# The end of a one-core encoder layer: its last layer norms written in a hand-made order on VectorE

## The chip, the core and the metric

The kernel runs on one core of one Trainium2 chip. TensorE multiplies matrices into PSUM, VectorE and ScalarE work on tiles of 128 partitions in SBUF, GpSimd issues gathers, and SyncE issues most of the transfers. The metric is the device time of one execution in microseconds. Lower is better.

## The reference

One encoder layer over 512 tokens of width 1024. The end of it is what matters here: a feed-forward part that picks 128 of 16384 experts for each token, a gated embedding, and a layer norm over their sum. Everything before is attention and routing.

```python
def layer_norm(x, g, b):
    mu = jnp.mean(xf, axis=-1, keepdims=True)
    var = jnp.mean(jnp.square(xf - mu), axis=-1, keepdims=True)
    y = (xf - mu) * lax.rsqrt(var + LN_EPS)
    return y * g + b
...
    # in peer_ffn, for each token:
    hpre = jnp.einsum('td,ted->te', xb, u_table[idx])
    act = g * jax.nn.gelu(hpre, approximate=False)
    return jnp.einsum('te,ted->td', act, v_table[idx])
...
    ffn = peer_ffn(h, ...)
    ple = gate * (p[i] @ ple_w[i])
    h = layer_norm(DN_ALPHA * h + ffn + ple, ln2_g, ln2_b)
```

## The kernel before

The 512 tokens are four chunks of 128 tokens, one on each partition. Chunk 0 computes its expert sum by gathers: GpSimd fetches single rows of the tables, VectorE weights them and adds them to `base[0]` (L1532 to L1536). Chunks 1 to 3 compute it as a dense product over all 16384 experts, in 128 blocks of 128 experts. TensorE adds each block into six PSUM tiles `acc[c][hf]`, one for each chunk (c = 0 to 2 for chunks 1 to 3) and half of 512 columns. For the three chunks `base[c]` is the tile `h`, which holds the rest of the sum.

A block n goes through these steps. SyncE loads 128 rows of the value table into `v_raw` or `raw` (`load_v`, L1487). Both are rings of three buffers. VectorE multiplies the gate weights `gt` by `ge` (L1598). Then `split` (L107) cuts values and weights into a high and a low part. ScalarE casts the high part (`hTh` or `whi` of the values, `a_hi` or a `raw` buffer of the weights), and VectorE subtracts it to get the low part (`hTl` or `wlo`, and `a_lo` or `raw`, all at L110). TensorE multiplies high by high, low by high and high by low (`expert_out`, L1546), 18 matmuls for a block over the six tiles. For the last four blocks, 124 to 127, the products are written behind the loop, tile by tile with all four blocks for each (L1631 to L1634).

In this loop the order on VectorE and SyncE is that of the program (`manual_schedule`). The order on TensorE and ScalarE is made by the scheduler, which puts ready instructions first by its own estimate. Each engine then runs its queue strictly in that order, and so does SyncE with its transfers.

Behind the loop stand the last norms, L1637 to L1650, in no `manual_schedule`, so that the scheduler mixes them with what stands before. For chunks 1 to 3 VectorE takes `acc` into `base` half by half with a running sum (L1646, a "take" below). Two small operations give the negative mean (L154, L155), ScalarE squares the row with that bias and sums it (L157), VectorE scales the sum (L158), ScalarE takes the root (L159), VectorE takes the reciprocal (L160) and refines it in four steps (L135 to L138). The row is weighted by the gain (L165) in place, and the last operation (L166) multiplies by the root's inverse and adds the bias row. Chunk 0 takes its mean and variance by two BN_STATS operations instead (L148 to L150, L163). Each chunk is then written to `out` by one transfer of 512 KB.

Of the kernel before, what the change touches and what calls it, by code (L numbers as in the profile page):

```python
# [9 lines left out]
F32 = mybir.dt.float32  # L10
# [4 lines left out]
AF = mybir.ActivationFunctionType  # L15
OP = mybir.AluOpType
# [3 lines left out]
D = 1024  # L20
# [7 lines left out]
EPS = 1e-5  # L28
# [33 lines left out]
GATS = 8  # L62
# [17 lines left out]
def tile_encoder_layer(ctx: ExitStack, tc: tile.TileContext, A: dict, out: bass.AP):  # L80
    nc = tc.nc
# [3 lines left out]
    small = ctx.enter_context(tc.tile_pool(name="small", bufs=4))  # L85
# [47 lines left out]
    def rsqrt_refine(y, y0, v, t):  # L133

        nc.vector.tensor_tensor(t, v, y0, op=OP.mult)  # L135
        nc.vector.tensor_tensor(t, t, y0, op=OP.mult)
        nc.vector.tensor_scalar(t, t, -0.5, 1.5, op0=OP.mult, op1=OP.add)
        nc.vector.tensor_tensor(y, t, y0, op=OP.mult)  # L138

    def layer_norm(r, g, b, sums=None, scr=None):  # L140

        ys = small.tile([128, 8], F32, name="ln_y")
        ve, sd, y0, y, t, ss = (ys[:, i:i + 1] for i in range(6))
        mu = small.tile([128, 2], F32, name="ln_mu")
        if sums is None:
            st = small.tile([128, 2, 6], F32, name="ln_st")
            for i in range(2):
                nc.vector.bn_stats(st[:, i, :], r[:, i * 512:(i + 1) * 512])  # L148
            nc.vector.bn_aggr(mu, st)
            nc.vector.tensor_scalar(ve, mu[:, 1:2], EPS, None, op0=OP.add)  # L150
            neg = None
        else:
            neg = mu[:, 1:2]
            nc.vector.tensor_tensor(neg, sums[:, 0:1], sums[:, 1:2], op=OP.add)  # L154
            nc.vector.tensor_scalar(neg, neg, -1.0 / D, None, op0=OP.mult)  # L155
            sq = wst.tile([128, D], F32, name="raw", bufs=3) if scr is None else scr
            nc.scalar.activation(sq, r, AF.Square, bias=neg, accum_out=ss)  # L157
            nc.vector.tensor_scalar(ve, ss, 1.0 / D, EPS, op0=OP.mult, op1=OP.add)  # L158
        nc.scalar.sqrt(sd, ve)  # L159
        nc.vector.reciprocal(y0, sd)  # L160
        rsqrt_refine(y, y0, ve, t)
        if neg is None:
            nc.vector.scalar_tensor_tensor(r, r, mu[:, 0:1], g, op0=OP.subtract, op1=OP.mult)  # L163
        else:
            nc.vector.scalar_tensor_tensor(r, r, neg, g, op0=OP.add, op1=OP.mult)  # L165
        nc.vector.scalar_tensor_tensor(r, r, y, b, op0=OP.mult, op1=OP.add)  # L166

    def row_bcast(pool, src, name, bufs=1):
        t = pool.tile([128, D], F32, name=name, bufs=bufs)
        nc.sync.dma_start(t, bass.AP(tensor=src.tensor, offset=src.offset, ap=[[0, 128], [1, D]]))  # L170
        return t
# [20 lines left out]
    at = pA.enter_context(tc.tile_pool(name="at", bufs=1))  # L192
# [580 lines left out]
    with tc.manual_schedule(engines={nc.tensor.engine}):  # L773
# [4 lines left out]
        norm = latent_k_norm(lat_k)  # L778
# [9 lines left out]
    lg = row_bcast(lnp, A["ln1_g"], "lg")  # L788
    lb = row_bcast(lnp, A["ln1_b"], "lb")
    ops = [ps_tile("mm"), ps_tile("mm"), ps_tile("pj"), ps_tile("pj")]  # L790
    for kk in range(4):
        w = stream(A["w_o"][kk * 256:(kk + 1) * 256, 0:512].rearrange("(k p) n -> p k n", p=128), [2, 512])
        for k2 in range(2):
            k = 2 * kk + k2
# [4 lines left out]
    for c in range(4):  # L799
        nc.vector.scalar_tensor_tensor(h[c][:, 0:512], h[c][:, 0:512], ALPHA, ops[c], op0=OP.mult, op1=OP.add,  # L800
                                       accum_out=rsum[c][:, 0:1])
# [5 lines left out]
    for c in range(4):  # L807
        cs = slice(c * 128, (c + 1) * 128)
        ps = ps_tile("pj")
        for k in range(8):  # L810
            mm3(ps, (aTh[:, k, cs], aTl[:, k, cs]), (w2h[:, k], w2l[:, k]), k == 0, k == 7)
        nc.vector.scalar_tensor_tensor(h[c][:, 512:1024], h[c][:, 512:1024], ALPHA, ps, op0=OP.mult, op1=OP.add,
                                       accum_out=rsum[c][:, 1:2])
# [16 lines left out]
    NGC, NDC = N_G // 128, N_D // 128  # L830
# [6 lines left out]
    base = [pB.tile([128, D], F32, name=f"base_{c}") if c < NGC else h[c] for c in range(4)]  # L837
# [3 lines left out]
    own_top = pB.tile([128, 4], F32, name="own_top")  # L841
# [100 lines left out]
    for g in range(16):  # L942
# [8 lines left out]
        if g:  # L951
            i, t = next(homes)
# [548 lines left out]
    pG = ctx.enter_context(tc.tile_pool(name="pG", bufs=1, reuse_waits="tile"))  # L1501
# [3 lines left out]
    acc = [[psA.tile([128, 512], F32, name=f"acc{c}{hf}") for hf in range(2)] for c in range(NDC)]  # L1505
# [47 lines left out]

    steps = list(gather_steps())
    late = []

    with tc.manual_schedule(engines={nc.vector.engine, nc.scalar.engine, nc.tensor.engine, nc.sync.engine,
                                     nc.gpsimd.engine}):
# [2 lines left out]
    done, spent = PRE, 0  # L1561
    held_a = []
    with tc.manual_schedule(engines={nc.vector.engine, nc.sync.engine}):
        for n, i in enumerate(order):
# [31 lines left out]
            a = gt[:, :, n % GB, :]  # L1596
# [31 lines left out]
            for f in steps[done:upto]:  # L1628
                f()
            done = upto  # L1630
        for c in range(NDC):  # L1631
            for hf in range(2):
                for x in late:
                    expert_out(x, c, (hf,))  # L1634


    turned.clear()  # L1637
    lg = row_bcast(pG, A["ln2_g"], "gat", GATS - 4)
    lb = row_bcast(pG, A["ln2_b"], "gat", GATS - 4)
    for c in range(4):  # L1640
        fsum = None
        if c >= NGC:
            fsum = small.tile([128, 2], F32, name="fsum", bufs=2)
            for hf in range(2):
                hs = slice(hf * 512, (hf + 1) * 512)
                nc.vector.scalar_tensor_tensor(base[c][:, hs], acc[c - NGC][hf],  # L1646
                                               own_top[:, 0:1] if c == NGC else 1.0, base[c][:, hs], op0=OP.mult,
                                               op1=OP.add, accum_out=fsum[:, hf:hf + 1])
        layer_norm(base[c], lg, lb, fsum, pG.tile([128, D], F32, name="gat_w", bufs=2))
        nc.sync.dma_start(out[c * 128:(c + 1) * 128, :], base[c])  # L1650


# [85 lines left out]
```

## Time and profile before

| | us |
|---|---|
| median of 3 runs | 1491.64 |
| lowest and highest run | 1488.11, 1492.6 |
| the profiled execution | 1489.54 |
| its span in the trace | 1487.8 |
| TensorE busy in the span | 1450.2 (97%) |
| VectorE busy in the span | 1268.5 (85%) |

Times in the trace count from the start of the span. The time of the profiled execution is 1.7 us more than its span. A row of the timeline gives start, duration, engine, line, operation, and in brackets the idle time before it with what ended it. Two instructions that don't depend on each other follow each other closer than their durations, so the step from one start to the next is what a row costs its engine.

### The profile page before, as it was taken

The page shows a single profiled execution, that of the slowest core. Times are in us where ns is not written, and L with a number is a line of the kernel's source. Part 1 is how long each engine was busy: PE and PEld are TensorE (multiplying, and loading weights), DVE is VectorE, ACT ScalarE, POOL GpSimd, SP SyncE. Part 2 cuts the span into 40 slices and gives each one's busy share as a digit, 9 for nine tenths or more (in the row PEclk, how much of TensorE's full clock was granted, in tenths as well). Part 3 has the DMA queues.
Part 4 walks back from the last instruction along what each step waited for, and adds up shares of the span by engine and source line. Part 5 has one row for each costly group of instructions (what it writes and reads, how often), then busy time and mean ns, then how long its engine had stood idle before and what let it go on. Part 6 is the DMA issues. An engine that isn't in the chain of part 4 may idle for free.

```text
span 1487.8 us, 22518 instructions
## 1 busy us (share of the span) xinstructions
PE 1450.2 (97%) x7693; PEld 1212.4 (81%) x7693; DVE 1268.5 (85%) x2736; ACT 638.4 (43%) x1203; POOL 570.7 (38%) x520
## 2 busy tenths in 40 slices
PE   9999999999999999999998999999999999999997
PEld 5788777788888878888887888988888888888775
DVE  7376786579998979998776987999899999999997
ACT  3355776243221554212555763444343333333433
POOL 1013110010014544344442435665555666666630
PEclk9999999999999999999999999999999999999999
DMA  7333340175239999999999999999999999999992
GB/s 255 99 111 92 97 128 30 29 245 170 100 125 351 334 416 415 405 324 336 392 416 410 376 396 369 415 417 417 401 393 411 412 412 411 412 412 412 411 362 85
DMA packets 196851, 453.82 MB, mean 305 GB/s; under 512 B 18945, under 2 KB 96897, under 8 KB 196738
## 3 DMA queue, kind: packets, MB, share of 16 engines
q1 hardware_dynamic: 119168, 211.72, 38.6%
q0 software_dynamic: 57984, 207.12, 35.5%
q10 hardware_dynamic: 19586, 33.57, 5.9%
q8 instruction: 60, 0.98, 0.2%
q14 instruction: 53, 0.43, 0.1%
HBM read 411.70 MB, written 37.75 MB: 302 GB/s over the span
## 4 chain that ended last, share of the span: by engine, by line
PE 56%; DMA 22%; DVE 9%; issue 6%; ACT 4%; POOL 3%; SPq 0%; ACTq 0%; DVEq 0%; POOLq 0%
PE acc L1551 16%; DMA raw<-in_v_rows_dram 11%; PE mm L1291 6%; PE hp L1291 5%; DMA ge_dram<-ge 4%; PE mm L129 4%; PE mm L131 4%; PE mm L130 4%; PE pj L129 3%; PE pj L130 3%; PE pj L131 3%; DMA v_raw<-in_v_rows_dram 3%; PE hp L129 1%; PE hp L131 1%; PE hp L130 1%
## 5 line engine op out<-in xcount | busy, mean ns | idle before, releaser
L110 DVE TENSOR_TENSOR wlo<-raw,whi 128x1024 fp32r<-128x1024 f32 (+4 forms) x113 | 131.5, 1164 | 45.7 <-ACT whi L110 45.4
L110 ACT CAST a_hi<-gt 128x384 fp32r<-128x384 f32 (+2 forms) x128 | 64.9, 509 | 242.4 <-DVE gt L1598 179.5
L110 ACT CAST whi<-raw 128x1024 fp32r<-128x1024 f32 (+4 forms) x113 | 113.0, 1001 | 106.9 <-PE mm L130 47.3
L1291 PE MATMUL mm<-whole,raw 128*128 128x256 f32 x672 | 153.1, 381 | 1.5 <-DMA raw<-in_uT_dram 1.5
L1174 POOL DMA_INDIRECT whi<-in_u_rows_dram,s_ix x51 | 64.2, 1259 | 218.5 <-DVE cand L994 129.7
L1551 PE MATMUL acc<-hTh,a_hi 128*128 128x512 f32 x456 | 141.8, 391 | 0.1
L1551 PE MATMUL acc<-hTl,a_hi 128*128 128x512 f32 x456 | 141.2, 390 | 0.0
L1551 PE MATMUL acc<-hTh,a_lo 128*128 128x512 f32 x456 | 140.9, 389 | 0.0
L1291 PEld LDWEIGHTS mm<-whole,raw 128*128 128x128 f32 x672 | 125.6, 190 | 17.9 <-DMA raw<-in_uT_dram 1.9
L1534 POOL DMA_INDIRECT gat<-in_v_rows_dram,i_sel x64 | 100.8, 1574 | 55.0 <-DVE base L1536 39.5
L110 ACT CAST hTh<-v_raw 128x1024 fp32r<-128x1024 f32 x74 | 77.8, 1051 | 55.9 <-PE acc L1551 23.1
L1551 PEld LDWEIGHTS acc<-hTl,a_hi 128*128 128x128 f32 x456 | 85.4, 188 | 18.3 <-DVE hTl L110 0.4
L1551 PEld LDWEIGHTS acc<-hTh,a_lo 128*128 128x128 f32 x456 | 85.4, 188 | 18.2 <-DVE a_lo L110 0.3
L1551 PEld LDWEIGHTS acc<-hTh,a_hi 128*128 128x128 f32 x456 | 84.1, 188 | 17.2 <-ACT a_hi L110 1.1
L110 DVE TENSOR_TENSOR hTl<-v_raw,hTh 128x1024 fp32r<-128x1024 f32 x74 | 90.2, 1219 | 6.4 <-ACT hTh L110 6.4
L1551 PE MATMUL acc<-wlo,a_hi 128*128 128x512 f32 x300 | 92.8, 390 | 0.2
L1551 PE MATMUL acc<-whi,a_hi 128*128 128x512 f32 x300 | 92.8, 391 | 0.1
L1551 PE MATMUL acc<-whi,a_lo 128*128 128x512 f32 x300 | 92.6, 390 | 0.0
L1174 POOL DMA_INDIRECT wlo<-in_u_rows_dram,s_ix x51 | 61.9, 1213 | 68.3 <-DVE s_dot L1176 56.0
L1519 POOL DMA_INDIRECT gat<-in_u_rows_dram,i_sel x52 | 69.1, 1329 | 45.2 <-DVE hdot L1525 34.1
L1536 DVE SCALAR_TENSOR_TENSOR base<-gat,hdot,base 128x1024 f32<-128x1024 f32 x64 | 82.0, 1281 | 1.0
L1273 ACT ACTIVATE ge<-mm 128x256 f32<-128x256 f32 x78 | 29.6, 380 | 110.4 <-PE mm L1291 100.5
(415 smaller groups left out, 3815.7 us busy)
## 6 DMA issues: line engine op xcount, KB each, us to landing
raw<-in_uT_dram SPq DMA_DIRECT2D x80, 512.0 KB, 7.8
v_raw<-in_v_rows_dram SPq DMA_DIRECT2D x78, 512.0 KB, 13.2
raw<-in_v_rows_dram SPq DMA_DIRECT2D x48, 512.0 KB, 13.8
g_dram<-g_st ACTq DMA_DIRECT2D x40, 512.0 KB, 12.1
ge_dram<-ge ACTq DMA_DIRECT2D x96, 128.0 KB, 7.0
ge<-ge_dram SPq DMA_DIRECT2D x96, 128.0 KB, 13.0
gt<-g_dram SPq DMA_DIRECT2D x30, 384.0 KB, 13.9
raw_u<-in_uT_dram SPq DMA_DIRECT2D x19, 512.0 KB, 7.8
```

The lines of the kernel that those rows point to most:

```text
L110: cut = nc.scalar.copy(hi, src), nc.vector.tensor_tensor(lo, src, r32(hi), op=OP.subtract)
L129: nc.tensor.matmul(ps, a[0], b[0], start=start, stop=False)
L130: nc.tensor.matmul(ps, a[0], b[1], start=False, stop=False)
L131: nc.tensor.matmul(ps, a[1], b[0], start=False, stop=stop)
L1174: nc.gpsimd.indirect_dma_start(out=u[:], out_offset=None, in_=u_rows, in_offset=bass.IndirectOffsetOnAxis(ap=ix[:, k:k + 1], axis=0))
L1273: nc.scalar.activation(ge, ps[:, :N_U], AF.Gelu)
L1291: nc.tensor.matmul(ps[:, :N_U], raw[:, k], whole[:, k, :], start=(k == 0), stop=(k == 7))
L1519: nc.gpsimd.indirect_dma_start(out=u[:], out_offset=None, in_=u_rows, in_offset=bass.IndirectOffsetOnAxis(ap=i_sel[:, c, k:k + 1], axis=0))
L1534: nc.gpsimd.indirect_dma_start(out=u[:], out_offset=None, in_=v_rows, in_offset=bass.IndirectOffsetOnAxis(ap=i_sel[:, c, k:k + 1], axis=0))
L1536: nc.vector.scalar_tensor_tensor(base[c], u, hdot[:, c, k:k + 1], base[c], op0=OP.mult, op1=OP.add)
L1551: nc.tensor.matmul(acc[c][hf], a[:, cs], b[:, hf * 512:(hf + 1) * 512], start=(n == 0 and i == 0), stop=(n == 127 and i == 2))
```

## The change

The first norm (chunk 0) becomes a generator, `first_norm`. The block loop calls one piece of it at the end of each of the iterations 124, 125 and 126, on engines whose order is written by hand. The first piece also loads the gain and bias rows, and the third issues chunk 0's write on SyncE.

The three other norms are written out under `manual_schedule` for VectorE: takes, means, weightings and roots of the chunks a, b, c (1, 2, 3) interleaved by hand. The weighting by the gain goes into other tiles (`gat_v`, `gat_w`) instead of in place. The small columns stand in one spare `gat` tile, so that the root and the refinement of a and b are one set of operations on two columns. The mean is one operation with a bias of two sums instead of two. The last chunk leaves in two halves of 512 columns, each with its own write of 256 KB.

```diff
+    def first_norm():
+        lg, lb = [row_bcast(pG, A[n], "gat", GATS - 4) for n in ("ln2_g", "ln2_b")]
...
+        for hf in range(2):
+            nc.vector.bn_stats(st[:, hf, :], r[:, hf * 512:(hf + 1) * 512])
+        nc.vector.bn_aggr(mu, st)
+        nc.vector.tensor_scalar(ys[:, 0:1], mu[:, 1:2], EPS, None, op0=OP.add)
+        nc.scalar.sqrt(ys[:, 1:2], ys[:, 0:1])
+        yield
+        nc.vector.scalar_tensor_tensor(r, r, mu[:, 0:1], lg, op0=OP.subtract, op1=OP.mult)
+        nc.vector.reciprocal(ys[:, 2:3], ys[:, 1:2])
+        rsqrt_refine(ys[:, 3:4], ys[:, 2:3], ys[:, 0:1], ys[:, 4:5])
+        yield
+        nc.vector.scalar_tensor_tensor(r, r, ys[:, 3:4], lb, op0=OP.mult, op1=OP.add)
+        nc.sync.dma_start(out[0:128, :], r)
+        yield
...
             for f in steps[done:upto]:
                 f()
             done = upto
+            if n >= 124:
+                assert done == len(steps)
+                next(norm, None)
...
+    def take(c, hf):
+        hs = halves[hf]
+        nc.vector.scalar_tensor_tensor(base[c][:, hs], acc[c - NGC][hf], own_top[:, 0:1] if c == NGC else 1.0,
+                                       base[c][:, hs], op0=OP.mult, op1=OP.add, accum_out=at(hf, c))
+    def means(c):
+        nc.vector.tensor_scalar(at(2, c), at(0, c), at(1, c), -1.0 / D, op0=OP.add, op1=OP.mult)
+        nc.scalar.activation(pG.tile([128, D], F32, name="gat_w", bufs=2), base[c], AF.Square, bias=at(2, c),
+                             accum_out=at(3, c))
+    def gains(c):
+        gained[c] = pG.tile([128, D], F32, name="gat_v" if c < 3 else "gat_w", bufs=2)
+        nc.vector.scalar_tensor_tensor(gained[c], base[c], at(2, c), lg, op0=OP.add, op1=OP.mult)
+    def root(c, n):
+        nc.vector.tensor_scalar(at(4, c, n), at(3, c, n), 1.0 / D, EPS, op0=OP.mult, op1=OP.add)
+        nc.scalar.sqrt(at(5, c, n), at(4, c, n))
+    def refine(c, n):
+        nc.vector.reciprocal(at(6, c, n), at(5, c, n))
+        rsqrt_refine(at(7, c, n), at(6, c, n), at(4, c, n), at(5, c, n))
+    def leave(c, cols):
+        t = gained[c][:, cols]
+        nc.vector.scalar_tensor_tensor(t, t, at(7, c), lb[:, cols], op0=OP.mult, op1=OP.add)
+        nc.sync.dma_start(out[c * 128:(c + 1) * 128, cols], t)
+    with tc.manual_schedule(engines={nc.vector.engine}):
+        a, b, c = range(NGC, 4)
+        take(a, 0)
+        take(a, 1)
+        means(a)
+        take(b, 0)
+        gains(a)
+        take(b, 1)
+        means(b)
+        gains(b)
+        root(a, 2)
+        take(c, 0)
+        refine(a, 2)
+        leave(a, slice(0, D))
+        take(c, 1)
+        means(c)
+        gains(c)
+        leave(b, slice(0, D))
+        root(c, 1)
+        refine(c, 1)
+        for hs in halves:
+            leave(c, hs)
```

The diff says nothing of TensorE, but the scheduler's order there changes too, behind the products of block 124. The tile names are `acc` with c, hf and a number. In the kernel before, this is where TensorE's queue comes to the last product of `acc00`, the one with `a_lo_13597` of block 127, and 41 matmuls of the other tiles stand behind it.

```order
L1551 MATMUL acc00_8458<-hTh_89,a_hi_13596 128x512 [waits Activation_49]
L1551 MATMUL acc01_8459<-hTh_89,a_hi_13596 128x512
L1551 MATMUL acc10_8460<-hTl_90,a_hi_13587 128x512
L1551 MATMUL acc00_8458<-hTl_90,a_hi_13596 128x512 [waits DVE_49]
L1551 MATMUL acc01_8459<-hTl_90,a_hi_13596 128x512
L1551 MATMUL acc00_8458<-hTh_89,a_lo_13597 128x512 [waits DVE_49]
L1551 MATMUL acc01_8459<-hTh_89,a_lo_13597 128x512
L1551 MATMUL acc10_8460<-hTh_89,a_lo_13588 128x512
```

In the changed kernel the products of block 127 (`a_hi_13616`, `a_lo_13617`) are TensorE's last 18, over all six tiles. These are the last twelve rows of the queue.

```order
L1551 MATMUL acc00_8458<-hTl_90,a_hi_13616 128x512 [waits DVE_49]
L1551 MATMUL acc01_8459<-hTl_90,a_hi_13616 128x512
L1551 MATMUL acc00_8458<-hTh_89,a_lo_13617 128x512 [waits DVE_49]
L1551 MATMUL acc01_8459<-hTh_89,a_lo_13617 128x512
L1551 MATMUL acc10_8460<-hTl_90,a_hi_13616 128x512
L1551 MATMUL acc10_8460<-hTh_89,a_lo_13617 128x512
L1551 MATMUL acc11_8461<-hTl_90,a_hi_13616 128x512
L1551 MATMUL acc11_8461<-hTh_89,a_lo_13617 128x512
L1551 MATMUL acc20_8462<-hTl_90,a_hi_13616 128x512
L1551 MATMUL acc20_8462<-hTh_89,a_lo_13617 128x512
L1551 MATMUL acc21_8463<-hTl_90,a_hi_13616 128x512
L1551 MATMUL acc21_8463<-hTh_89,a_lo_13617 128x512
```

So `acc00` is complete with 9 matmuls behind it now. On SyncE the queue before ends with the loads of blocks 125, 126 and 127 and the four writes:

```order
L1489 DMA v_raw<-in_v_rows_dram 128x1024 [waits DMAHW2_49,DVE_49]
L1489 DMA v_raw<-in_v_rows_dram 128x1024 [waits DMAHW3_49,DVE_49]
L1489 DMA v_raw<-in_v_rows_dram 128x1024 [waits DMAHW6_49,DMAHW4_49,DVE_49]
L1650 DMA out_dram<-base_3028 128x1024 [waits DMAHW5_49,DVE_49]
L1650 DMA out_dram<-h_86 128x1024 [waits DVE_49]
L1650 DMA out_dram<-h_87 128x1024 [waits DMAHW7_49,DVE_49]
L1650 DMA out_dram<-h_88 128x1024 [waits DMAHW0_49,DVE_49]
```

In the changed kernel SyncE's queue ends like this:

```order
L1489 DMA v_raw<-in_v_rows_dram 128x1024 [waits DMAHW2_49,DVE_49]
L1489 DMA v_raw<-in_v_rows_dram 128x1024 [waits DMAHW3_49,DVE_49]
L1577 DMA out_dram<-base_3028 128x1024 [waits DMAHW4_49,DVE_49]
L1489 DMA v_raw<-in_v_rows_dram 128x1024 [waits DMAHW6_49,DMAHW5_49,Activation_49]
L1700 DMA out_dram<-gat_v 128x1024 [waits DVE_49]
L1700 DMA out_dram<-gat_v 128x1024 [waits DMAHW7_49,DVE_49]
L1700 DMA out_dram<-gat_w 128x512 [waits DMAHW0_49,DVE_49]
L1700 DMA out_dram<-gat_w 128x512 [waits DMAHW1_49,DVE_49]
```

Chunk 0's write, which waits for the end of the first norm, has moved ahead of the load of block 127. On VectorE the changed queue stands like this from the low parts of block 125 to those of block 127, with the first norm (L1572 to L1576) between:

```order
L110 TENSOR_TENSOR raw<-gt_13358,raw 128x384 [waits DVE_49]
L1572 SCALAR_TENSOR_TENSOR base_3028<-base_3028,ln_mu,gat 128x1024 [waits DMAHW0_49]
L1573 RECIPROCAL ln_y<-ln_y 128x1
L135 TENSOR_TENSOR ln_y<-ln_y 128x1 [waits DVE_49]
L136 TENSOR_TENSOR ln_y<-ln_y 128x1 [waits DVE_49]
L137 TENSOR_SCALAR ln_y<-ln_y 128x1 [waits DVE_49]
L138 TENSOR_TENSOR ln_y<-ln_y 128x1 [waits DVE_49]
L1623 TENSOR_TENSOR gt_13358<-gt_13358,ge 128x8x32 [waits DMAHW5_49]
L110 TENSOR_TENSOR hTl<-v_raw,hTh 128x1024 [waits DMAHW3_49]
L110 TENSOR_TENSOR a_lo<-gt_13358,a_hi 128x384 [waits Activation_49]
L1576 SCALAR_TENSOR_TENSOR base_3028<-base_3028,ln_y,gat 128x1024 [waits DMAHW1_49]
```

In the kernel before, the whole first norm stood ahead of the low parts of block 125. It was spread over the work of the blocks 122 to 124.

## Rows read from the trace of the kernel before

**Rows 1.** Busy time by engine in three stretches of the end; clock, DMA share.

```profile
1460.00:1470.00 10.00, 10.00 (x44) 7.50 (x43) 8.15 (x14) 3.93 (x6) 0.00 (x0) 1.00 0.26 101
1470.00:1478.00 8.00, 7.56 (x34) 5.93 (x32) 6.53 (x23) 2.89 (x6) 0.00 (x0) 1.00 0.15 63
1478.00:1484.00 6.00, 0.00 (x0) 0.00 (x0) 5.61 (x16) 1.45 (x3) 0.00 (x0) 0.87 0.22 91
```

**Rows 2.** Chain that ended last, by time: start, length, engine, tile, line.

```profile
1443.46 24.82 PE acc L1551 x103
```

**Rows 3.** Timeline: start, us, engine, line, operation; chunk 1's take and norm.

```profile
1467.88 0.85 PE L1551 MATMUL acc<-hTh,a_lo 128*128 128x512 f32 x3
1468.31 0.75 DVE L1646 SCALAR_TENSOR_TENSOR h<-acc,own_top,h 128x512 f32<-128x512 f32 x1 [0.75 <-PE acc L1551]
...
1468.98 0.74 DVE L1646 SCALAR_TENSOR_TENSOR h<-acc,own_top,h 128x512 f32<-128x512 f32 x1
...
1471.97 0.15 DVE L158 TENSOR_SCALAR ln_y<-ln_y 128x1 f32<-128x1 f32 x1 [1.36 <-ACT gat_w L157]
1472.04 1.27 DVE L165 SCALAR_TENSOR_TENSOR h<-h,ln_mu,gat 128x1024 f32<-128x1024 f32 x1
...
1473.23 0.15 DVE L160 RECIPROCAL ln_y<-ln_y 128x1 f32<-128x1 f32 x1
```

**Rows 4.** Timeline of the last chunk, from TensorE's last matmul on.

```profile
1477.17 0.39 PE L1551 MATMUL acc<-hTh,a_lo 128*128 128x512 f32 x1
1477.20 0.68 DVE L1646 SCALAR_TENSOR_TENSOR h<-acc,h 128x512 f32<-128x512 f32 x1
...
1477.87 0.69 DVE L1646 SCALAR_TENSOR_TENSOR h<-acc,h 128x512 f32<-128x512 f32 x1
...
1480.31 0.15 DVE L158 TENSOR_SCALAR ln_y<-ln_y 128x1 f32<-128x1 f32 x1
...
1480.50 0.20 ACT L159 ACTIVATE ln_y<-ln_y 128x1 f32<-128x1 f32 x1 [0.22 <-DVE ln_y L158]
1481.58 0.15 DVE L160 RECIPROCAL ln_y<-ln_y 128x1 f32<-128x1 f32 x1
1481.77 0.16 DVE L135 TENSOR_TENSOR ln_y<-ln_y 128x1 f32<-128x1 f32 x1
...
1482.54 1.28 DVE L166 SCALAR_TENSOR_TENSOR h<-h,ln_y,gat 128x1024 f32<-128x1024 f32 x1
```

**Rows 5.** Timeline of the last four blocks, all engines.

```profile
1458.72 0.33 SPq L1489 DMA_DIRECT2D v_raw<-in_v_rows_dram  x1
...
1460.11 0.62 PE L1551 MATMUL acc<-whi,a_lo 128*128 128x512 f32 x2
...
1460.90 1.05 ACT L110 CAST whi<-v_raw 128x1024 fp32r<-128x1024 f32 x1
1460.92 0.34 SPq L1650 DMA_DIRECT2D out_dram<-base  x1
...
1463.60 0.42 DVE L1598 TENSOR_TENSOR gt<-gt,ge 128x256 f32<-128x256 f32 x1
...
1463.93 1.22 DVE L110 TENSOR_TENSOR hTl<-v_raw,hTh 128x1024 fp32r<-128x1024 f32 x1
...
1464.47 1.05 ACT L110 CAST hTh<-v_raw 128x1024 fp32r<-128x1024 f32 x1
...
1465.87 1.22 DVE L110 TENSOR_TENSOR hTl<-v_raw,hTh 128x1024 fp32r<-128x1024 f32 x1
...
1467.01 0.55 DVE L110 TENSOR_TENSOR a_lo<-gt,a_hi 128x384 fp32r<-128x384 f32 x1
```

**Rows 6.** Tile view of `v_raw` in 1438 to 1470 us.

```profile
DMA to landing us min/median/max: 3.2/4.2/6.3
```

**Rows 7.** DMA issues: tiles, queue, count, KB each, median us to landing.

```profile
out_dram<-h SPq DMA_DIRECT2D x3, 512.0 KB, 2.6
ple_dram<-pl SPq DMA_DIRECT2D x4, 256.0 KB, 2.3
```

More of the change, by code (lines that the diff above doesn't have):

```diff
@@ L1555, in tile_encoder_layer @@
     late = []
+    gains_in = []
+    def first_norm():
+        lg, lb = [row_bcast(pG, A[n], "gat", GATS - 4) for n in ("ln2_g", "ln2_b")]
+        gains_in.extend((lg, lb))
+        r = base[0]
+        ys = small.tile([128, 8], F32, name="ln_y")
+        mu = small.tile([128, 2], F32, name="ln_mu")
+        st = small.tile([128, 2, 6], F32, name="ln_st")
+        for hf in range(2):
[11 more added lines that the diff above has]
+        yield
+    norm = first_norm()
     with tc.manual_schedule(engines={nc.vector.engine, nc.scalar.engine, nc.tensor.engine, nc.sync.engine,
@@ L1637, in tile_encoder_layer @@
     turned.clear()
[L1638 to L1650, printed above, removed]
+    lg, lb = gains_in
@@ new lines, in tile_encoder_layer, with at @@
+    st = pG.tile([128, D], F32, name="gat", bufs=GATS - 4)[:, 0:32].rearrange("p (k c) -> p k c", c=4)
+    halves = [slice(hf * 512, (hf + 1) * 512) for hf in range(2)]
+    gained = {}
+    def at(k, c, n=1):
+        return st[:, k, c - NGC:c - NGC + n]
+    def take(c, hf):
+        hs = halves[hf]
+        nc.vector.scalar_tensor_tensor(base[c][:, hs], acc[c - NGC][hf], own_top[:, 0:1] if c == NGC else 1.0,
+                                       base[c][:, hs], op0=OP.mult, op1=OP.add, accum_out=at(hf, c))
```

## The prediction, made before the changed kernel ran

> **What bounds the kernel now.** I read the end backwards. From 1478 to 1484 us TensorE does nothing and VectorE is busy 5.61 of 6.00 us [rows 1], so the last stage is VectorE's, with a write behind it. From 1460 to 1470 TensorE is busy 10.00 of 10.00 us [rows 1]. The chain that ended last says where the one hands over to the other: it runs 24.82 us through TensorE from 1443.46 [rows 2], and then goes to VectorE's first take at 1468.31, which had waited for `acc` [rows 3]. The matmul that released it began at 1467.88 (the first of a row of three, each 0.39 long, about 0.23 apart) [rows 3]. TensorE's last matmul begins at 1477.17 [rows 4]. So VectorE starts on the norms some 9 us before TensorE has done, and its tail overlaps the rest of the products: it runs from 1468.31 to the end of the last row, 1482.54 + 1.28 = 1483.82 [rows 3, 4]. That is 15.51 us, of which 1.36 are a wait for ScalarE's squares [rows 3]. The span ends at 1487.8, so 3.98 us lie behind VectorE, for the last write. The reader is to see that two things set the end: when `acc00` is complete, and how long VectorE's tail is from there.
>
> **The tail itself, step by step.** Steps are from one start to the next. A take of chunk 1 steps 0.67 (1468.31 to 1468.98) [rows 3]. A take of the others steps 0.60 (1477.20 to 1477.87 is 0.67, with a small operation of 0.07 between) [rows 4]. A weighting of 128x1024 steps 1.19 (1472.04 to 1473.23), and a small operation on which nothing next depends 0.07 (1471.97 to 1472.04) [rows 3]. Reciprocal and refinement are five dependent steps in 1482.54 - 1481.58 = 0.96 us [rows 4]. The written order then costs:
> six takes, 2 x 0.67 + 4 x 0.60 = 3.74;
> three weightings and two whole leaves, 5 x 1.19 = 5.95;
> two refinements, 1.92 (the joint root of a and b does on two columns what two did, so one of three is saved, about 0.9 us of instructions);
> the last leave in two halves, taken as two takes of the same size, 1.28;
> three means with the wait for the running sum, about 0.8 (one operation where there were two);
> two roots, 0.14;
> and two waits, 0.1 for the squares of b behind its weighting, and 0.35 for the last root. Before, that root (1480.50, 0.20 long) lay beside a weighting that ended in the reciprocal at 1481.58 [rows 4]. Now it stands behind all other work, so it is exposed.
> The sum is 14.3 us against 15.51. The tail is 1.2 us shorter from its first take. The last root, uncovered, takes back nearly half of what the joint one gives. The bounds are 13.8 (no wait at all) and 15.0 (four more steps between dependent operations of 0.19 each, where I took none).
>
> **The last write.** Half of the row is written while the other half is computed, and the last transfer is 256 KB instead of 512. Writes of 512 KB to `out` land in 2.6 us, one of 256 KB in 2.3 [rows 7]. I take 0.4 off, between 0 and 0.7 (half of the computation of the row). [...] The trace has no write in halves to show it.
>
> **When the tail starts.** This is the large term, and the diff doesn't show it. TensorE's order changed: before, 41 matmuls stand behind the one that completes `acc00`; now 9. The scheduler sees block 127's weights come late on a VectorE that carries the first norm ahead of them, and puts all 18 products of that block last. If TensorE ran without a stall it would start block 124 as before at 1460.11 + 2 x 0.23 = 1460.57 [rows 5]. The row that completes `acc00` is the 63rd from there, so it begins 62 x 0.23 = 14.3 later at 1474.8 and ends 0.39 later at 1475.2 [rows 3]. The first take then starts at 1475.3, 7.0 us later than now.
>
> But block 127 is late by itself too. Its load was issued at 1458.72, ahead of chunk 0's write at 1460.92 [rows 5]. Now the write stands ahead of it on SyncE and waits for the end of the first norm, which VectorE reaches only after block 126. The cast `whi` of block 125 began at 1460.90, after TensorE had left block 123's `whi` at 1460.11 + 0.62 [rows 5]. Nothing in the change moves this, since both casts use the same ring. So VectorE comes to the end of block 125 as before, at 1463.60 [rows 5], where `gt` of block 126 began. From there:
> the first norm's weighting and refinement, 1.19 + 0.76 + 0.07 = 2.0, to 1465.6;
> `gt` 0.33, `hTl` 1.14 (1465.87 to 1467.01), `a_lo` 0.5 [rows 5], to 1467.6;
> the norm's last operation 1.28, to 1468.9;
> the write's issue on SyncE 0.4 (0.34 long [rows 5]), so the load of block 127 is issued at 1469.3, 10.6 us later than now.
> A load of `v_raw` lands in 3.2, 4.2 or 6.3 us (least, median, most) [rows 6]. No row shows one right behind a write. I take the median, since the write is ahead of it on the queue as the loads of other rows are, and keep both ends. [...] The value lands at 1473.5, ScalarE's cast takes 1.05 (as at 1464.47), to 1474.6; then VectorE needs 1.14 and 0.55 for `hTl` and `a_lo` [rows 5], or TensorE 8 x 0.23 for the products ahead of the one that completes `acc00`. Both come to about 1.8, and the matmul itself to 0.4. The first take starts at 1476.8, 8.5 us later than now. With landings of 3.2 and 6.3 it is 1475.8 and 1478.9.
> Who waits: behind the load on SyncE only writes, behind ScalarE's cast of block 127 the squares, behind VectorE's `hTl` all takes. VectorE stands idle from about 1469.3 to 1474.6, so the first norm that was moved there is free but the tail behind it isn't. After the first take TensorE is done in 9 x 0.23, or 2.1 us, and VectorE wants the last half 8 us later, so no other take waits.
>
> **The sum.** 8.5 later, 1.2 shorter, 0.4 less at the write: +6.9 us. Against the profiled execution's own 1489.54 that is 1496.4, against the median of the runs 1498.5. The three runs and the profiled one have a mean of 1490.5, and I put the difference on that: 1497.4.
>
> **Rivals.**
> *The load is on time* (the write is no obstacle, or the transfer is short): TensorE's order alone decides, first take at 1475.3, 7.0 - 1.2 - 0.4 = +5.4, 1495.9. For it: the least landing is 3.2 [rows 6] with nothing else on the queues then. Against it: the issue time itself hangs on VectorE.
> *The load is slower*: 6.3, +9.0, 1499.5. At the end few transfers run (DMA share 0.15 from 1470) [rows 1], which speaks against it.
> *Not slower: the change does as it reads.* If `acc00` is complete when VectorE is through with its blocks, at 1468.3, the shorter tail and write count alone: -1.6 us, 1488.9, within 0.3%. It decides wherever the first take starts before some 1472. Against it: TensorE runs its queue in order, and 62 matmuls of 0.23 cannot be passed in less than 14 us.
> *A part is given back*: VectorE's tail is at its lower bound of 13.8, TensorE is through the blocks earlier since ScalarE no longer waits for the first root ahead of block 123's cast, and the sum falls to about +3.5, 1494.0.
> *Faster by more than 0.3%* would take 4.5 us, three times what the tail saves in all.
>
> **How the numbers follow.** About 0.3%, or 4.5 us, is what a measurement of this kernel can tell from no change. Chances: forecast 0.58, load on time 0.16, slower load 0.08, does as it reads 0.07, part given back 0.08, faster by another way 0.03. The forecast and the two loads are slower by over 0.3%, except where run-to-run spread (1488.11 to 1492.6) or a small stall takes the difference under 4.5, for which I take 0.07 off: slower 0.75. Same: 0.07 + 0.07 + 0.08 = 0.22. Faster 0.03. The range goes from the part given back, less half of the spread of runs, to the slow load with some of it: 1492.8 to 1500.8. It leaves out the reading as it stands and the faster case, and little above.
>
> **What would show it.** In the profile of the changed kernel: the first take at 1475 to 1479 instead of 1468.31; VectorE idle for 4 to 6 us between the first norm's last operation and `hTl` of block 127; the load of block 127 issued right behind chunk 0's write, near 1469; TensorE waiting for the cast of block 127 before its last 18 products; a tail of 14 to 15 us from first take to last leave, with an idle piece ahead of the last reciprocal; and the span's end some 3.6 us behind VectorE. I am wrong if the first take starts before 1473, or if the tail from there is under 12 us.

## The result: slower by 1.25%, most of it in the block loop

| | before | after |
|---|---|---|
| median of 5 runs each, same chip (us) | 1488.74 | 1509.01 |
| lowest and highest run | 1487.89, 1492.6 | 1507.01, 1509.32 |
| the profiled execution, its span | 1489.54, 1487.8 | 1509.16, 1507.4 |

The ratio is 1.0125, with a 95% interval of 1.0113 to 1.0138. The forecast was slower, 1497.4 in a range of 1492.8 to 1500.8. The direction is right, and the size is about three times what was forecast: the span is 19.6 us longer where 6.9 were expected.

The end looks as it was foretold, but all of it stands late. The chain of waits of the changed kernel (start, length, what) ends like this:

```profile
1399.84 71.38 PE acc L1551 x306
...
1481.85 3.94 DMA v_raw<-in_v_rows_dram
1485.81 1.05 ACT hTh L110
...
1486.91 2.38 PE acc L1551 x9
...
1489.31 1.44 DVE h L1677 x4
...
1502.60 0.75 DVE gat_w L1699
```

Before, one run of TensorE work led to the first take [rows 2]. Now the load of block 127 stands in the chain, then its cast, then nine matmuls that have to wait for it. The timeline of the changed kernel (start, us, engine, line, operation, idle before) shows the same places as [rows 3 to 5]:

```profile
1473.18 0.39 PE L1551 MATMUL acc<-whi,raw 128*128 128x512 f32 x1
...
1476.11 1.28 DVE L1572 SCALAR_TENSOR_TENSOR base<-base,ln_mu,gat 128x1024 f32<-128x1024 f32 x1
...
1480.09 1.28 DVE L1576 SCALAR_TENSOR_TENSOR base<-base,ln_y,gat 128x1024 f32<-128x1024 f32 x1
...
1481.40 0.34 SPq L1577 DMA_DIRECT2D out_dram<-base  x1
1481.85 0.37 SPq L1489 DMA_DIRECT2D v_raw<-in_v_rows_dram  x1
...
1486.89 1.23 DVE L110 TENSOR_TENSOR hTl<-v_raw,hTh 128x1024 fp32r<-128x1024 f32 x1 [5.18 <-ACT hTh L110]
1486.91 1.67 PE L1551 MATMUL acc<-hTh,a_hi 128*128 128x512 f32 x6 [0.73 <-ACT hTh L110]
...
1489.31 0.75 DVE L1677 SCALAR_TENSOR_TENSOR h<-acc,own_top,h 128x512 f32<-128x512 f32 x1 [0.73 <-PE acc L1551]
...
1501.39 0.20 ACT L1691 ACTIVATE gat<-gat 128x1 f32<-128x1 f32 x1 [1.28 <-DVE gat L1690]
1501.63 0.16 DVE L1694 RECIPROCAL gat<-gat 128x1 f32<-128x1 f32 x1 [0.27 <-ACT gat L1691]
...
1502.60 1.41 DVE L1699 SCALAR_TENSOR_TENSOR gat_w<-gat_w,gat 128x512 f32<-128x512 f32 x2
1503.38 0.99 SPq L1700 DMA_DIRECT2D out_dram<-gat_w  x2
```

The first row is the first matmul of block 124 that the change left in its place. Before, it stood at 1460.57, by the row at 1460.11 [rows 5]. From these starts the 19.6 us divide:

| stretch | before | after | difference |
|---|---|---|---|
| span's start to the loop's first matmul into `acc` | 893.3 | 895.0 | +1.7 |
| from there to block 124 | 567.3 | 578.2 | +10.9 |
| block 124 to the first take | 7.74 | 16.13 | +8.4 |
| first take to VectorE's end | 15.51 | 14.70 | -0.8 |
| VectorE's end to the span's end | 3.98 | 3.39 | -0.6 |

The last three rows are the terms of the prediction. They come to +7.0, and 6.9 were forecast. What was missed stands ahead of all code that the diff touches. The start of the loop lies between 891.0 and 895.9 in the profiles of this study, in kernels with the same order of instructions too, so the 1.7 us of the first row can't be put down to the change. The 10.9 us can be seen in TensorE's rate. The busy time by engine from 1150 to 1400 us, first of before, then of after (columns: stretch, length, busy time and count of PE, PEld, DVE, ACT, POOL; granted clock; DMA share; GB/s):

```profile
1150.00:1400.00 250.00, 249.77 (x1098) 204.73 (x1097) 243.33 (x284) 94.51 (x134) 162.12 (x102) 1.00 1.04 412
```

```profile
1150.00:1400.00 250.00, 250.00 (x1073) 201.43 (x1072) 240.70 (x280) 92.84 (x134) 159.67 (x101) 1.00 1.04 404
```

TensorE is busy throughout in both, at a granted clock of 1.00, so neither waits nor the clock make the difference. It does 1073 matmuls where it did 1098: 0.233 us for one instead of 0.227. The loop has 124 x 18 = 2232 of them ahead of block 124, and 0.0055 us more for each is 12 us, about the 10.9 found. The operation's group on the two pages (busy, mean ns | idle) says the same, 389 ns before and 395 after:

```profile
L1551 PE MATMUL acc<-hTh,a_lo 128*128 128x512 f32 x456 | 140.9, 389 | 0.0
```

```profile
L1551 PE MATMUL acc<-hTh,a_lo 128*128 128x512 f32 x456 | 144.0, 395 | 0.0
```

### The profile page after: what moved, and what is told of

Read it like the earlier page. It is cut to its first block, busy times and chain, and to the rows that moved or that the text cites. A ratio compares the mean times of both kernels' runs of the same rounds, so it can differ in the third digit from the quotient of the medians.

```text
span 1507.4 us, 22511 instructions
## 1 busy us (share of the span) xinstructions
PE 1464.9 (97%) x7693; PEld 1215.3 (81%) x7693; DVE 1270.9 (84%) x2728; ACT 637.9 (42%) x1202; POOL 569.4 (38%) x520
## 4 chain that ended last, share of the span: by engine, by line
PE 72%; DVE 10%; DMA 6%; issue 5%; POOL 4%; ACT 3%; SPq 0%; ACTq 0%; DVEq 0%; POOLq 0%
PE acc L1551 35%; PE mm L1291 7%; PE mm L129 3%; PE mm L130 3%; PE mm L131 3%; DMA ge_dram<-ge 3%; PE hp L1291 3%; PE pj L129 3%; PE pj L130 3%; PE pj L131 3%; POOL wlo L1174 1%; POOL whi L1174 1%; PE hp L129 1%; PE hp L131 1%; PE hp L130 1%
## 5 line engine op out<-in xcount | busy, mean ns | idle before, releaser
L1551 PE MATMUL acc<-hTh,a_lo 128*128 128x512 f32 x456 | 144.0, 395 | 0.0
L110 DVE TENSOR_TENSOR hTl<-v_raw,hTh 128x1024 fp32r<-128x1024 f32 x74 | 90.3, 1221 | 12.6 <-ACT hTh L110 12.6
L110 DVE TENSOR_TENSOR a_lo<-gt,a_hi 128x384 fp32r<-128x384 f32 (+2 forms) x128 | 69.8, 546 | 17.8 <-ACT a_hi L110 17.7
```

Of the source, the lines that this page charges most:

```text
L110: cut = nc.scalar.copy(hi, src), nc.vector.tensor_tensor(lo, src, r32(hi), op=OP.subtract)
L1551: nc.tensor.matmul(acc[c][hf], a[:, cs], b[:, hf * 512:(hf + 1) * 512], start=(n == 0 and i == 0), stop=(n == 127 and i == 2))
```

## Experiments on the loop: where the tiles lie

The order of the loop's instructions is the same in both kernels. What differs is addresses. Before, the running sums of the takes went into the tile `fsum` of the pool `small`, two buffers to which the program gives 32 bytes of each partition. The changed kernel keeps its sums in a `gat` tile and has no `fsum`. The tiles that are allocated behind that pool, on what I call the left side (`h`, the values `hTh`, `hTl`, `whi`, `wlo`, the `raw` ring, `ge`, `gat`), therefore all begin 64 bytes lower: `hTh` at byte 34752 of a partition instead of 34816, a multiple of 256. The tiles allocated from the other end, the right side (the weights `a_hi` and `a_lo`, `v_raw`), stay: `a_hi` at 163840. A matmul of the loop takes its values from the left and its weights from the right. The kernel has spacers for both sides, `GAP_SMALL` and `GAP_EDGE` in units of 4 bytes (L72), so that the places can be moved alone.

**after_gap** is the changed kernel with the 64 bytes put back. **before_m64** and **before_m256** are the kernel before with the left side 64 and 256 bytes lower, and nothing else changed.

```diff
after_gap      -GAP_SMALL, GAP_EDGE, ... = 96, 216, ...   +... = 112, 216, ...
before_m64     -GAP_SMALL, GAP_EDGE, ... = 96, 216, ...   +... = 80, 216, ...
before_m256    -GAP_SMALL, GAP_EDGE, ... = 96, 216, ...   +... = 32, 216, ...
```

> The changed kernel with GAP_SMALL 112 for 96. The changed kernel no longer has the two small sums tiles (fsum, 2 x 32 bytes a partition), so all tiles allocated behind that pool lie 64 bytes lower than in the kernel before; 16 more floats in the gap put them back, with the same instruction order on every engine as the changed kernel. Theory A (place of the tiles): the matmuls of the block loop step 0.227 us again instead of 0.233, block 124 begins near 1460.6 instead of 1473, the first take comes at 1476 to 1477, and the time is 6 to 8 us over the kernel before (1495 to 1497), which is what the steps of the prediction gave. Rival B (the code itself, its waits or the order at the end slow the loop): the step stays 0.233 and the time 1507 to 1509.

> The kernel before with GAP_SMALL 80 for 96: the same instructions in the same order on all engines, the tiles behind the small pool 64 bytes lower, as in the changed kernel. Theory A: the block loop's matmuls step 0.233, the loop is 10 to 11 us longer, the whole 11 to 13 us slower than before (1500 to 1501). Rival B: no change, within 0.3%.

> The kernel before with GAP_SMALL 32 for 96: the same tiles 256 bytes lower. If it is the tiles' place within 128 or 256 bytes that counts, the step stays 0.227 and the time is that of before. If it is the place within a larger unit (the rows of the value tiles are 2048 bytes for each matmul, and start at multiples of 2048 bytes in the kernel before), the step is 0.233 or more and the time 1500 or more.

after_gap takes 1496.32 us, a ratio of 1.005 (1.0034 to 1.0066). before_m64 takes 1502.33, 1.009 (1.0067 to 1.0113). before_m256, in a single run, takes 1490.83 beside 1488.48 of before. The same stretch of the loop, of after_gap, of before_m64 and of before_m256:

```profile
1150.00:1400.00 250.00, 250.00 (x1101) 205.58 (x1100) 243.75 (x285) 93.75 (x134) 164.21 (x102) 1.00 1.04 411
```

```profile
1150.00:1400.00 250.00, 250.00 (x1073) 201.41 (x1072) 241.31 (x280) 92.05 (x133) 160.45 (x102) 1.00 1.04 404
```

```profile
1150.00:1400.00 250.00, 250.00 (x1102) 205.85 (x1101) 243.99 (x285) 94.28 (x136) 163.49 (x102) 1.00 1.04 412
```

The changed kernel with its tiles put back does 1101 matmuls and reaches block 124 at 1460.25. The kernel before with its tiles moved does 1073, as the changed kernel does, and reaches it at 1472.57. So the loop's loss is the 64 bytes, with the code of the end having no part in it. It is not the move as such either: with 256 bytes the stretch holds 1102 matmuls, and the single run's time lies within those of before (1486.17 to 1493.87).

Is it the place of the left side, or where the two sides lie to each other? **before_edge** moves the right side alone by 64 bytes, **both_m64** both sides by 64, **before_m128** the left by 128.

```diff
before_edge    -GAP_SMALL, GAP_EDGE, ... = 96, 216, ...   +... = 96, 200, ...
both_m64       -GAP_SMALL, GAP_EDGE, ... = 96, 216, ...   +... = 80, 232, ...
before_m128    -GAP_SMALL, GAP_EDGE, ... = 96, 216, ...   +... = 64, 216, ...
```

> The kernel before with GAP_EDGE 200 for 216: the tiles on the right side, among them the weights a_hi and a_lo that TensorE loads, lie 64 bytes higher; the values that stream past them stay. If the streamed values' place is what counts, the step stays 0.227 and the time is that of before. If the loaded weights' place counts too, the step is longer, up to 0.233, and the time up to 1500.

> The kernel before with GAP_SMALL 80 and GAP_EDGE 232: the streamed values and the loaded weights both lie 64 bytes lower than in the kernel before, so that they lie to each other as there. Theory A1 (it is the place of the two to each other that counts): the step is 0.227 and the time that of before, 1488 to 1491. Rival A2 (each has to start at a multiple of 128 bytes by itself): the step is 0.233 or longer, the time 1500 or more.

> The kernel before with GAP_SMALL 64: the left tiles, the streamed values among them, 128 bytes lower. If the unit is 128 bytes: step 0.227, 1488 to 1491. If it is 256 bytes: 0.233 or longer, 1500 or more.

Single runs: before_edge 1498.04, both_m64 1505.12, before_m128 1496.21. In the same stretch before_edge does 1073 matmuls in 250.00 us busy, and before_m128 1078. From the loop's first matmul to block 124 before_edge needs 578.2 us, as the changed kernel and before_m64 do; its time is lower because its loop begins early, at 891.0. both_m64 is another case. Its timeline of TensorE (three rows of two matmuls each), and that of before_m64:

```profile
1190.34 0.61 PE L1551 MATMUL acc<-hTh,a_lo 128*128 128x512 f32 x2
1190.79 0.62 PE L1551 MATMUL acc<-hTh,a_hi 128*128 128x512 f32 x2
1191.25 0.62 PE L1551 MATMUL acc<-hTl,a_hi 128*128 128x512 f32 x2
```

```profile
1190.24 0.63 PE L1551 MATMUL acc<-hTl,a_hi 128*128 128x512 f32 x2
1190.70 0.63 PE L1551 MATMUL acc<-hTh,a_lo 128*128 128x512 f32 x2
1191.17 0.63 PE L1551 MATMUL acc<-whi,a_hi 128*128 128x512 f32 x2
```

With both sides moved alike two matmuls take 0.455 us again, 0.227 each. With one moved they take 0.465. So in these runs the rate follows where the sides lie to each other. A rival is that the transfers hold up the matmuls. The last blocks of the changed kernel bear on it, with the busy times of two stretches and four starts of TensorE:

```profile
1477.00:1479.00 2.00, 2.00 (x10) 1.51 (x9) 1.86 (x8) 0.39 (x1) 0.00 (x0) 1.00 0.00 0
1480.00:1482.00 2.00, 2.00 (x10) 1.63 (x9) 1.71 (x3) 0.20 (x1) 0.00 (x0) 1.00 0.00 0
```

```profile
1477.05 0.39 PE L1551 MATMUL acc<-wlo,raw 128*128 128x512 f32 x1
...
1478.64 0.61 PE L1551 MATMUL acc<-whi,raw 128*128 128x512 f32 x2
...
1480.45 0.62 PE L1551 MATMUL acc<-hTh,a_lo 128*128 128x512 f32 x2
...
1482.08 0.40 PE L1551 MATMUL acc<-wlo,raw 128*128 128x512 f32 x1
```

From 1480.45 to 1482.08 seven matmuls take 0.233 us each while the transfers move 0 GB/s, so the slow step there is not made by transfers. From 1477.05 to 1478.64 seven take 0.227 each, in the same kernel at the same granted clock of 1.00. These belong to the blocks 124 and 125, whose weights lie in `raw`, on the left like their values. That fits the place of values and weights to each other, but doesn't prove it: other matmuls of these two blocks take 0.23 or more in the changed kernel, and in the kernel before some do too, just behind a wait (0.47 for two from 1462.82).

But both_m64 is still slower than before, for another reason. Its stretch of the loop, and two groups of its waits (engine and who is waited for: us, times, longest):

```profile
1150.00:1400.00 250.00, 241.61 (x1041) 193.71 (x1041) 233.64 (x273) 90.76 (x130) 158.07 (x98) 0.99 1.03 394
```

```profile
PEld acc L1551 <- ACT a_hi L110: 12.0, 10, 3.8
...
PE acc L1551 <- ACT a_hi L110: 7.9, 3, 3.4
```

TensorE is busy for 241.61 of 250.00 us and waits for weights, and the transfers run at 394 GB/s instead of 412 at nearly the same share of the DMA engines (1.03 and 1.04). That the transfers make the weights late is argued from these rates and not shown wait by wait. This was a guess to be tested: that tiles off multiples of 128 bytes slow the transfers. **both_m128** puts both sides on odd multiples of 128, **before_edge256** moves the right by 256, **before_m32** the left by 32.

```diff
both_m128      -GAP_SMALL, GAP_EDGE, ... = 96, 216, ...   +... = 64, 248, ...
before_edge256 -GAP_SMALL, GAP_EDGE, ... = 96, 216, ...   +... = 96, 152, ...
before_m32     -GAP_SMALL, GAP_EDGE, ... = 96, 216, ...   +... = 88, 216, ...
```

> The kernel before with GAP_SMALL 64 and GAP_EDGE 248: streamed values and loaded weights both 128 bytes lower, so that they lie to each other as before. The run with both 64 lower had the short step of 0.227, but waited for loads at 392 to 397 GB/s, where the kernel before has 412, and took 1505. Theory A (tiles that start off a multiple of 128 bytes make the transfers slower): step 0.227, 410 GB/s or more from 1150 to 1350, 1488 to 1491. Rival B (any move of both sides does it, or that run was disturbed for another reason): either 400 GB/s or less here as well, or the same time for another cause than the place; with B 1496 to 1505.

> The kernel before with GAP_EDGE 152: the right tiles, the loaded weights among them, 256 bytes higher. If the step goes by the place of values and weights to each other within 256 bytes: 0.227 and 1487 to 1491. If it goes by 512 bytes or more: 0.230 or longer, 1496 or more.

> The kernel before with GAP_SMALL 88: the left tiles 32 bytes lower, the smallest move the pools allow. By the steps so far (64 lower 0.233, 128 lower 0.231, 256 lower 0.227) the move of 32 bytes lengthens the step too, to 0.229 to 0.234, and the time is 1494 to 1503; if a unit of 64 bytes is all that counts, the step stays 0.227, and the time 1488 to 1491.

Single runs: both_m128 1510.08, before_edge256 1491.66, before_m32 1500.89. The same stretch of both_m128:

```profile
1150.00:1400.00 250.00, 240.45 (x1026) 195.01 (x1025) 232.21 (x270) 90.30 (x131) 154.43 (x98) 0.97 1.03 393
```

The guess fell: both_m128 loses its transfer rate as well, with 393 GB/s. Its mean granted clock is 0.97 there, so a part of its loss may be the clock's. before_edge256 does 1100 matmuls at 412 GB/s, as before does, and before_m32 1073. Of all placements:

| left, right moved by (bytes) | matmuls in the stretch | one matmul (us) | GB/s |
|---|---|---|---|
| 0, 0 | 1098 | 0.227 | 412 |
| -256, 0 and 0, +256 | 1102, 1100 | 0.227 | 412, 412 |
| -32, 0 and -64, 0 | 1073, 1073 | 0.233 | 404, 404 |
| 0, +64 | 1073 | 0.233 | 408 |
| -128, 0 | 1078 | 0.232 | 404 |
| -64, -64 and -128, -128 | 1041, 1026, with waits | 0.227 | 394, 393 |

One effect is shown, then: a matmul takes 0.232 to 0.233 us where one side alone is moved by 32, 64 or 128 bytes, and 0.227 where none is, where one is moved by 256, or where both are moved alike (several runs of after, after_gap and before_m64, one of each other placement). A second was seen in two single runs: the transfers run at 394 and 393 GB/s instead of 412 where both sides are moved, by 64 and by 128. Neither was seen at 256, where one side alone was moved: 0.227 us and 412 GB/s. Where TensorE never waits its own rate may set the GB/s: in before_m64 it is busy for 250.00 of 250.00 us. So these rows show only that the transfers could do at least this much.

The cause of the slower transfers isn't shown. In before_m64 some four fifths of the bytes land 64 lower as well (the gathers, `raw`, `ge`, half of `gt`; an estimate from the issues of the stretch in the kernel before), and it moved 404 GB/s.

The records of single packets say which transfers lose. One of 4096 bytes takes 159 ns (mean, same stretch) in the kernel before, in the gathers and in the loads alike. It takes 163 and 162 in before_m64, 167 and 165 in both_m64, 166 and 166 in both_m128. So gathers and loads lose about alike, though the gathers' targets lie at the same places in before_m64 and in both_m64.

## Experiments on the end

**after_gap_write** is after_gap with chunk 0's write issued behind the loop, so that the load of block 127 no longer stands behind it.

```diff
-        nc.sync.dma_start(out[0:128, :], r)
         yield
...
     turned.clear()
+    nc.sync.dma_start(out[0:128, :], base[0])
```

> The changed kernel with its tiles put back in place (GAP_SMALL 112), and chunk 0's write issued behind the loop instead of in its iteration 126, so that on SyncE the load of block 127 stands ahead of it again. Theory A (the write ahead of the load is what delays block 127 and made the scheduler put its products last): the load is issued near 1455 to 1459 instead of 1468.92, acc00 is complete with 27 matmuls behind it instead of 9, the first take comes near 1471 instead of 1476.24, and the time is 4 to 6 us under the run with GAP_SMALL 112 alone, 1490 to 1492. Rival B (the load was hidden, TensorE would have been as late anyway since the first norm holds VectorE): under 1 us better, 1495 to 1496.

It takes 1492.4 us, 1.0019 (1.0007 to 1.003) of before. In after_gap the timeline has the late load and what follows:

```profile
1468.47 0.34 SPq L1577 DMA_DIRECT2D out_dram<-base  x1
1468.92 0.37 SPq L1489 DMA_DIRECT2D v_raw<-in_v_rows_dram  x1
...
1472.75 1.05 ACT L110 CAST hTh<-v_raw 128x1024 fp32r<-128x1024 f32 x1 [3.37 <-DMA v_raw<-in_v_rows_dram]
1473.83 1.23 DVE L110 TENSOR_TENSOR hTl<-v_raw,hTh 128x1024 fp32r<-128x1024 f32 x1 [5.05 <-ACT hTh L110]
1473.85 1.66 PE L1551 MATMUL acc<-hTh,a_hi 128*128 128x512 f32 x6 [0.72 <-ACT hTh L110]
...
1476.24 0.75 DVE L1677 SCALAR_TENSOR_TENSOR h<-acc,own_top,h 128x512 f32<-128x512 f32 x1 [0.72 <-PE acc L1551]
```

In after_gap_write all three loads are issued by 1457, and the first take starts 3.7 us earlier:

```profile
1445.17 11.80 SPq L1489 DMA_DIRECT2D v_raw<-in_v_rows_dram  x3
1469.85 0.34 SPq L1665 DMA_DIRECT2D out_dram<-base  x1
...
1472.51 0.75 DVE L1677 SCALAR_TENSOR_TENSOR h<-acc,own_top,h 128x512 f32<-128x512 f32 x1 [0.75 <-PE acc L1551]
```

So the place of one write is worth 4 to 5 us: 3.9 between the two medians (1496.32 - 1492.4), and 4.6 by the two ratios, each to the runs of before that were taken with it. It acts through the scheduler too: with the load early, 27 matmuls stand behind the one that completes `acc00` instead of 9. Before had 41, and its first take came 4.2 us earlier still [rows 3]. The two causes, late data and TensorE's order, can't be had apart by this edit, since the one moves the other.

**tail_only** is the kernel before with the written tail alone. The first norm stays where it was, in one piece behind the loop's code, and TensorE's order is that of before. `GAP_SMALL` is 112, so that the tiles stay too.

```diff
+    layer_norm(base[0], lg, lb, None, pG.tile([128, D], F32, name="gat_w", bufs=2))
+    nc.sync.dma_start(out[0:128, :], base[0])
...
+    with tc.manual_schedule(engines={nc.vector.engine}):
+        a, b, c = range(NGC, 4)
+        take(a, 0)
...
+            leave(c, hs)
```

> Only the end of the change: the three norms written out under the hand-made order, tiles put back in place (GAP_SMALL 112), but the first norm and its write behind the loop as in the kernel before, with the same order on TensorE as the kernel before. Theory A: first take at 1468.3 as before; the takes of b and c now wait for TensorE (c's second half is complete only at 1477.6), so the tail doesn't get the 0.8 us that its instructions save, ends near 1483.8 as before, and only the halves of the last write give 0.5: -0.5 us, 1488.0 with the kernel before at 1488.5. Rival B: the tail is worth its shorter list, -1.5 to -2 us, 1486.5 to 1487.

It takes 1488.54, 0.9995 (0.9982 to 1.0007): no difference that can be measured. The timeline of VectorE shows why the shorter program brings nothing there:

```profile
1467.63 0.75 DVE L1652 SCALAR_TENSOR_TENSOR h<-acc,own_top,h 128x512 f32<-128x512 f32 x1 [0.75 <-PE acc L1551]
...
1471.50 0.69 DVE L1652 SCALAR_TENSOR_TENSOR h<-acc,h 128x512 f32<-128x512 f32 x1 [0.39 <-PE acc L1551]
...
1474.22 0.69 DVE L1652 SCALAR_TENSOR_TENSOR h<-acc,h 128x512 f32<-128x512 f32 x1 [0.29 <-PE acc L1551]
...
1480.82 0.16 DVE L1669 RECIPROCAL gat<-gat 128x1 f32<-128x1 f32 x1 [0.27 <-ACT gat L1666]
...
1481.79 1.41 DVE L1674 SCALAR_TENSOR_TENSOR gat_w<-gat_w,gat 128x512 f32<-128x512 f32 x2
```

VectorE reaches two takes before TensorE has their sums and waits 0.39 and 0.29 us, and it waits 0.27 for the last root. The tail is 1481.79 + 1.41 - 1467.63 = 15.57 us, and it was 15.51. The halves of the write do count here, 3.3 us behind VectorE instead of 3.98.

**tail_root** issues the last root ahead of chunk b's leave, so that the leave covers it.

```diff
         gains(c)
-        leave(b, slice(0, D))
         root(c, 1)
+        leave(b, slice(0, D))
         refine(c, 1)
```

> The run tail_only with one exchange: the last chunk's root (its scaling on VectorE and the root on ScalarE) stands ahead of chunk b's last operation, which then covers it. Theory A: the 0.27 us idle piece ahead of the last reciprocal goes, the tail from the first take to the last half ends 0.3 to 0.4 us earlier relative to the last take, and the time is 0.3 to 0.4 us under tail_only, which its interval against the kernel before cannot tell from no change (0.9975 to 1.0005). Rival B: the root has to wait for the squares on VectorE's queue and holds the operation behind it: no gain, or 0.1 us lost.

It takes 1489.47, 1.0 (0.9986 to 1.0013). The wait is gone from the timeline of VectorE:

```profile
1478.29 0.68 DVE L1652 SCALAR_TENSOR_TENSOR h<-acc,h 128x512 f32<-128x512 f32 x1
...
1480.60 0.15 DVE L1665 TENSOR_SCALAR gat<-gat 128x1 f32<-128x1 f32 x1
1480.67 1.28 DVE L1674 SCALAR_TENSOR_TENSOR gat_v<-gat_v,gat 128x1024 f32<-128x1024 f32 x1
1481.86 0.15 DVE L1669 RECIPROCAL gat<-gat 128x1 f32<-128x1 f32 x1
...
1482.82 1.41 DVE L1674 SCALAR_TENSOR_TENSOR gat_w<-gat_w,gat 128x512 f32<-128x512 f32 x2
```

From the last take to the last leave it needs 4.53 us, tail_only from 1477.03 needed 4.76. The 0.23 are there in the stage and too small for the median. No version of this study is faster than before by an amount that its runs can tell from none.

## Why the prediction was wrong

**The step that failed** is the one that reads "If TensorE ran without a stall it would start block 124 as before at 1460.11 + 2 x 0.23 = 1460.57". It was 1473.18. The sum goes by VectorE and the load, and the same fault stands there: "So VectorE comes to the end of block 125 as before, at 1463.60". The next operation, the first norm's L1572, began at 1476.11, and at 1463.27 in after_gap, where the tiles lie as before. TensorE did run without a stall (250.00 of 250.00 us in the stretch above), but at 0.233 us for a matmul. The prediction carried the loop over unchanged because no instruction in it moved, and it listed what the change removes by instructions alone. It didn't list the tile that goes, nor what lies behind that tile. No rival held it either, so the range was too low as a whole. after_gap, which has the change without the move of tiles, takes 1496.32, against a forecast of 1497.4, and 7.8 us more than the runs of before taken with it, against 6.9. The terms of the end come nearer still, +7.0, but that is partly luck: the tail was put 0.4 too short and the write's gain 0.2 too small, which cancel in part.

**TensorE's order and the late load** were right. In after everything stands 12.6 us later than the prediction had it (1473.18 - 1460.57), and from that base: the load's issue was put at 1469.3, and is at 1481.85, 1469.24 on the old base. The first take was put at 1476.8, and 1489.31 is 1476.70. VectorE's idle time ahead of block 127's `hTl` was put at 4 to 6 us, and is 5.18. In after_gap, without such a shift, the load is issued at 1468.92 and the first take starts at 1476.24.

**The landing** was taken as 4.2 us, the median of [rows 6]. It is 3.94 in the chain of after, between the least of those rows, 3.2, and their median. Loads and casts were late by as much as said, but TensorE felt little of that: it had other products until 1486.2 and was idle for 0.73 us.

**The tail** was put at 14.3 us and is 14.70 (14.69 in after_gap). The two halves of the last leave take 1.41 instead of 1.28. The three means, from the step behind each second take to the next operation, cost 0.25, 0.37 and 0.37 instead of 0.8 in all. The last root was put at 0.07 and 0.35 of waiting, and from its start to the reciprocal it is 0.42 (1501.21 to 1501.63, of which 0.27 idle). tail_only adds what the prediction didn't say: the gain needs TensorE to be through early enough. There two takes wait for it; here none does behind the first, since the first take is late and only 9 matmuls follow it.

**The write in halves** was put at -0.4 and gave -0.6 (3.98 to 3.39; 3.3 in tail_only). The issues in after show the first half leaving at 1503.38, 0.6 before VectorE's end at 1504.01.

**The rival that the change does as it reads** gave -1.6 us. It needs TensorE's old order, and moving the first norm is what lost this order. tail_only keeps it, and its median shows no difference. Its profile has a span of 1486.5 instead of 1487.8, but of these 1.3 us 0.7 are an earlier first take (1467.63), ahead of all that the edit touches, and 0.7 the write. The 1.2 that the tail was to give are not there.

## What to carry to other kernels

In this kernel a tile that went moved every tile allocated behind it, and a loop that the diff doesn't touch changed its rate, from 0.227 us a matmul to 0.233 for 64 bytes. So compare the addresses of the hot tiles along with the order of instructions (here a move of one side by 256 bytes kept the 0.227), and put a spacer back before the change is judged. A write that stood ahead of a load in SyncE's queue cost 4 to 5 us here: the load was issued at 1468.92, 0.45 us behind it, in after_gap, and by 1457 in after_gap_write. Such a wait is priced by who waits for the load, and by what the scheduler makes of the load being late. A tail that is shorter in instructions is worth only what its input lets it be: 15.57 us in tail_only, where it waits for TensorE, against 15.51 before.

## What the runs showed of the hardware

- One fp32r matmul of 128x512 steps 0.227 us where values and weights lie to each other as before, or one side is moved by 256 bytes within the partition, and 0.233 where one is moved by 32 or 64 (0.232 by 128), at a granted clock of 1.00 each time. With both sides moved alike it steps 0.227 too, at 0.99 and 0.97. Over the loop 0.233 for 0.227 is 11 us of 1489. In the changed kernel seven steps of 0.233 stand in a stretch where the transfers move 0 GB/s. Which unit causes it isn't shown. All tiles of a side move together in these edits, so it isn't shown either that it is values against weights. A matmul of the loop reads one of each side, and seven steps of 0.227 in the changed kernel, with both on the left, fit it.
- With both sides moved by 64 or 128 the transfers run at 394 and 393 GB/s instead of 412, with the DMA engines as busy (1.03 and 1.04), and TensorE waits for its weights. Each of these is a single run. Gathers and loads lose about alike: 159 ns for a packet of 4096 bytes before, 167 and 165 in both_m64. The cause isn't shown: with the left side alone moved by 64 most targets are moved too, and 404 were reached.
- A load issued 0.45 us behind a write of 512 KB on the same queue landed in 3.94 us (the changed kernel, 1481.40 and 1481.85).
